# A PEER layer on Trainium2: 160 instead of 128 tokens served by gathered expert rows, and one of the gate products on ScalarE

## The chip, the cores and the metric

The kernel runs on one core of one Trainium2 chip. The metric is device time in microseconds (us) of one execution: the median of three runs of the kernel before is 2171.63 us (2168.15 to 2172.48). A profiled execution of the same kernel gives the trace that is read here.

## The reference, cut to what matters

The reference is one layer of a decoder over 576 tokens that count at the end (512 of a prompt, 64 of eight samples): a gated delta rule and an mLSTM side by side, then a product-key expert layer (PEER), then a norm. The change lies in the expert layer:

```
def block(xb):                                    # 128 tokens
    qh = einsum('td,de->te', xb, w_query).reshape(128, 8, 2, 128)
    s = einsum('thpd,hpnd->thpn', qh, sub_keys)   # 8 heads, 2 halves, 128 keys
    sv, si = top_k(s, 16)
    cand = sv[:, :, 0, :, None] + sv[:, :, 1, None, :]
    top_s, pos = top_k(cand, 16)                  # 16 of 16384 experts a head
    gate = softmax(top_s)
    act = gelu(einsum('thkd,td->thk', expert_u[eidx], xb))
    return einsum('thk,thkd->td', gate * act, expert_v[eidx])
```

Each token picks 8 x 16 = 128 experts; an expert is one row of `expert_u` and one of `expert_v`, 1024 numbers of four bytes each.

## The kernel before

**Two ways for one layer.** Most tokens (ND = 448) go *densely*: TensorE multiplies all 16384 rows of `u` with them, ScalarE takes the Gelu, VectorE multiplies with a gate matrix that is zero for the experts not chosen, and TensorE multiplies the result with all rows of `v`. The last NG = 128 tokens go *by gathered rows*: they lie on the 128 partitions, GpSimd fetches for each the row of its rank-c expert (one indirect DMA of 512 KB a rank, for `u` and again for `v`: 256 gathers), and VectorE takes the dot product with the token (L1225) or adds gate times row to the sum (L1231, tile `yt`).

**The dense loop.** 128 blocks of experts are walked twice, once in `hidden` with `u` (tile `pz`) and once in `experts` with `v` (tile `py`). One step of either loop is called a *half* here: 24 matmuls, that is 8 chunks of D by three products of split numbers (hi by hi, hi by lo, lo by hi: `mm3`, L132 to L134), each with a 128x128 weight and ND columns. Halves 0 to 127 are `hidden`, 128 to 255 `experts`. For each half SP fetches a weight block (`wr`, 512 KB, seven halves ahead), ScalarE makes its high part (`uh`, in `hi`) and VectorE its low part (`ul`, in `lo`); in `hidden` ScalarE takes the Gelu of `pz` (`gz`). In `experts` VectorE multiplies two halves of `gz` with the gates `wj` (L1374) and splits the product (L1381), in alternate halves.

**The gates.** `select` finds the chosen experts of a block of 128 tokens on VectorE, by a long chain of small instructions. `onehots` then builds, for eight tokens (an *octet*, index q), four one-hot arrays `oh[0..3]` of 128 x (8 x 128) on VectorE: two comparisons and two products, high and low part of the gate. `scatter` multiplies them on TensorE with 16 small matmuls (tile `pw`), `stored` copies the result on ScalarE (`wst`) and SP writes it to HBM (`wd`), from where `gates` loads it as `wj`. The array tiles have two buffers each, so octet q needs the matmuls of octet q-2 to be done.

**Order.** From the first half on, PE, DVE, ACT and SP each run strictly in the order in which the program writes their instructions (`in_order`). What VectorE does beside `lo` is dealt out by `fill`: every half gives a credit (HALF less WL for `lo`), from which gathers (1.3 each, as many as `gcred` allows) and pieces of `select` and `onehots` (the number behind `yield`) are paid. Work put off by n halves goes through `later` and `run_due`.

**The end.** After the last half, `gather_out` norms the gathered tokens on VectorE; then the last two blocks of `v` are multiplied one output chunk d at a time, VectorE adds each chunk to `y`, ScalarE squares it and GpSimd adds up five of the squares (`rms_add`), and the dense tokens are normed and written.

## Time and profile before

| | |
|---|---|
| profiled execution, device time | 2175.39 us |
| its span, first to last instruction | 2173.6 us, granted clock 0.986 |
| median of three runs | 2171.63 us |
| TensorE (PE) busy | 2115.0 us, 97% of the span |
| VectorE (DVE) busy | 1561.8 us, 72% |
| ScalarE (ACT) busy | 803.4 us, 37% |
| `hidden`, first matmul to first of `experts` | 807.7 to 1522.6 us |
| `experts`, first to last matmul | 1522.6 to 2157.7 us |

The busy share of PE counts the full length of each matmul, and they overlap; how dense the stream is shows only in the distance from start to start. The shares of DVE, ACT and DMA are means over stages that differ, so they are read by stage.

### The profile page before, as it was taken

The page shows a single profiled execution, that of the slowest core. Times are in us where ns is not written, and L with a number is a line of the kernel's source. Part 1 is how long each engine was busy: PE and PEld are TensorE (multiplying, and loading weights), DVE is VectorE, ACT ScalarE, POOL GpSimd, SP SyncE. Part 2 cuts the span into 40 slices and gives each one's busy share as a digit, 9 for nine tenths or more (in the row PEclk, how much of TensorE's full clock was granted, in tenths as well). Part 3 has the DMA queues.
Part 4 walks back from the last instruction along what each step waited for, and adds up shares of the span by engine and source line. Part 5 has one row for each costly group of instructions (what it writes and reads, how often), then busy time and mean ns, then how long its engine had stood idle before and what let it go on. Part 6 is the DMA issues. An engine that isn't in the chain of part 4 may idle for free.

```text
span 2173.6 us, 33670 instructions
## 1 busy us (share of the span) xinstructions
PE 2115.0 (97%) x12800; PEld 1934.0 (89%) x12800; DVE 1561.8 (72%) x2985; ACT 803.4 (37%) x1217; POOL 539.2 (25%) x423
## 2 busy tenths in 40 slices
PE   8999999999999998999998899999999999999997
PEld 7898999889998998999997799999899999999996
DVE  6676665675557888897885687777887767676764
ACT  5533333343244452334433335433323232323222
POOL 1101000210014552110110121035543334333321
PEclk9999999999999999999999899999999999999999
DMA  6353333556455355767865577789999999999971
GB/s 240 121 161 100 101 104 99 159 158 213 152 163 175 117 193 197 258 209 253 289 232 218 209 246 263 282 313 370 362 387 338 318 330 321 327 320 331 314 259 44
DMA packets 236638, 502.32 MB, mean 231 GB/s; under 512 B 29764, under 2 KB 125764, under 8 KB 232764
## 3 DMA queue, kind: packets, MB, share of 16 engines
q1 hardware_dynamic: 199468, 365.93, 50.0%
q0 software_dynamic: 36864, 134.23, 17.5%
q8 instruction: 100, 1.64, 0.3%
q14 instruction: 62, 0.51, 0.1%
q10 hardware_dynamic: 144, 0.01, 0.0%
HBM read 419.05 MB, written 81.05 MB: 230 GB/s over the span
## 4 chain that ended last, share of the span: by engine, by line
PE 59%; DVE 2%; DMA 0%; issue 0%; ACT 0%; POOL 0%; DVEq 0%; POOLq 0%; ACTq 0%
PE py L132 10%; PE py L134 10%; PE py L133 10%; PE pz L134 9%; PE pz L132 9%; PE pz L133 9%; PE pw L1170 2%; DVE ul L1297 1%; DMA gr<-in_ur,gi 0%; DVE eq L1084 0%; DVE yo L1443 0%; DVE oh L1154 0%; DVE oh L1151 0%; DVE ti L976 0%; DVE ti L980 0%
## 5 line engine op out<-in xcount | busy, mean ns | idle before, releaser
L134 PE MATMUL pz<-x2h,ul 128*128 128x448 f32 x1024 | 380.5, 372 | 19.6 <-DVE ul L1297 19.6
L132 PE MATMUL pz<-x2h,uh 128*128 128x448 f32 x1024 | 384.2, 375 | 0.0
L133 PE MATMUL pz<-x2l,uh 128*128 128x448 f32 x1024 | 379.1, 370 | 0.0
L132 PE MATMUL py<-ah,uh 128*128 128x448 f32 x1024 | 376.3, 368 | 0.6 <-ACT gk L1347 0.6
L133 PE MATMUL py<-al,uh 128*128 128x448 f32 x1024 | 376.2, 367 | 0.0
L134 PE MATMUL py<-ah,ul 128*128 128x448 f32 x1024 | 376.2, 367 | 0.0
L1297 DVE TENSOR_TENSOR ul<-wr,uh 128x1024 fp32r<-128x1024 f32 x256 | 311.9, 1218 | 35.4 <-ACT uh L1291 34.5
L1291 ACT ACTIVATE uh<-wr 128x1024 fp32r<-128x1024 f32 x256 | 269.3, 1052 | 174.9 <-issue 170.2
L1222 POOL DMA_INDIRECT gr<-in_v,gi x128 | 192.4, 1503 | 454.6 <-DVE yt L1231 291.5
L1222 POOL DMA_INDIRECT gr<-in_ur,gi x128 | 188.8, 1475 | 463.4 <-DVE gr L1225 254.1
L132 PE MATMUL acc<-xnh,wh 128*128 128x296 f32 (+1 forms) x768 | 233.6, 304 | 7.2 <-ACT xnh L283 6.2
L133 PE MATMUL acc<-xnl,wh 128*128 128x296 f32 (+1 forms) x768 | 233.9, 305 | 0.5 <-DVE xnl L284 0.5
L134 PE MATMUL acc<-xnh,wl 128*128 128x296 f32 (+1 forms) x768 | 233.1, 305 | 0.0
L134 PEld LDWEIGHTS pz<-x2h,ul 128*128 128x128 f32 x1024 | 195.8, 191 | 39.0 <-DVE ul L1297 22.2
L132 PEld LDWEIGHTS py<-ah,uh 128*128 128x128 f32 x1024 | 191.5, 187 | 21.1 <-ACT gk L1347 1.0
L132 PEld LDWEIGHTS pz<-x2h,uh 128*128 128x128 f32 x1024 | 196.0, 191 | 15.9
L133 PEld LDWEIGHTS pz<-x2l,uh 128*128 128x128 f32 x1024 | 195.8, 191 | 15.5
L134 PEld LDWEIGHTS py<-ah,ul 128*128 128x128 f32 x1024 | 191.5, 187 | 20.1
L133 PEld LDWEIGHTS py<-al,uh 128*128 128x128 f32 x1024 | 191.5, 187 | 20.1
L127 ACT ACTIVATE wh<-wr 128x1024 fp32r<-128x1024 f32 x104 | 110.0, 1058 | 213.5 <-issue 78.1
L1330 ACT ACTIVATE gz<-pz 128x448 f32<-128x448 f32 x118 | 64.1, 543 | 318.6 <-PE pz L134 318.6
L1381 DVE TENSOR_TENSOR al<-gz,ah 128x896 fp32r<-128x896 f32 x59 | 64.5, 1093 | 154.0 <-ACT ah L1376 154.0
(405 smaller groups left out, 3712.9 us busy)
## 6 DMA issues: line engine op xcount, KB each, us to landing
wr<-in_u SPq DMA_DIRECT2D x128, 512.0 KB, 5.6
wr<-in_v SPq DMA_DIRECT2D x128, 512.0 KB, 5.2
gz<-gz SPq DMA_DIRECT2D x112, 448.0 KB, 3.9
wd<-wst SPq DMA_DIRECT2D x28, 1024.0 KB, 6.3
wj<-wd SPq DMA_DIRECT2D x112, 256.0 KB, 5.3
wr<-in_w_in SPq DMA_DIRECT2D x48, 512.0 KB, 3.9
wr<-in_w_q SPq DMA_DIRECT2D x32, 512.0 KB, 3.5
wr<-in_w_out SPq DMA_DIRECT2D x16, 512.0 KB, 4.9
```

Source lines behind the costliest of these rows:

```text
L127: self.last_hi = self.nc.scalar.activation(hi, src, AF.Copy)
L132: mm(out, wh, xh, start=start, stop=False)
L133: mm(out, wh, xl, start=False, stop=False)
L134: self.last_mm = mm(out, wl, xh, start=False, stop=stop)
L1170: nc.tensor.matmul(pw[:, u, :], oh[0][:, t], oh[2 + x][:, t], start=x == 0, stop=x == 1)
L1222: nc.gpsimd.indirect_dma_start(out=t, out_offset=None, in_=src, in_offset=bass.IndirectOffsetOnAxis(ap=self.gi[:, x, c:c + 1], axis=0))
L1291: self.nc.scalar.activation(w, self.raws[s], AF.Copy)
L1297: self.nc.vector.tensor_sub(w, self.raws.pop(s), self.ws[s][0].bitcast(F32))
L1330: nc.scalar.activation(*todo, AF.Gelu)
L1381: nc.vector.tensor_sub(al, z, ah.bitcast(F32))
```

## The change

160 tokens instead of 128 go by gathered rows, 416 instead of 448 densely. The 32 added tokens (NX) lie four times on the partitions; each copy takes a quarter (XK = 32) of the 128 ranks, so 2 x 32 more gathers of 512 KB do it. For this `xt`, `yt`, `gi`, `ga` exist twice; the transposes of `ffn_sink` also bring the 32 tokens into place, four-fold; `select` of block 1 (now tokens 320 to 447) sends its indices to the second `gi` by four SP DMAs; `gather_out` adds up the four partial sums and norms both parts. The low-part gate product `oh[3]` moves from VectorE (one instruction for eight tokens) to ScalarE (eight instructions, one a token, the gate as a scale per partition), at the start of `scatter`, which comes one half after `onehots` instead of two. A ScalarE copy `sx` spreads an operand of the product in `select` over its full size. The weights' high parts are made three halves ahead instead of two. The numbers that set the order change: HALF 4.8 to 4.55 with SCAT 0.9 more in a half that scatters an octet, MUL 1.1 to 1.0, GQ0 (gathers a half in most of `hidden`) 0.65 to 1.1.

```diff
-NG = 128
+NX = 32
+XG = P // NX
+XK = PH * TOPK // XG
+NG = P + NX
-TBLK = [(t, min(P, ND - t)) for t in range(0, ND, P)]
+TBLK = [(NT - 2 * P, P), (0, P), (P, P), (2 * P, NT - 4 * P)]
-HALF = 4.8
-WL, MUL = 1.2, 1.1
+HALF, SCAT = 4.55, 0.9
+WL, MUL = 1.2, 1.0
-GQ0, GQ1, GQ2, GTAIL = 0.65, 2.0, 1.7, 3
+GQ0, GQ1, GQ2, GTAIL = 1.1, 2.0, 1.7, 3
...
@@ ffn_sink
+                for x, (dst, v, a) in enumerate(((self.xt, t, w - NG), (self.yt, self.y[k], ND))):
+                    if k % 2 == 0:
+                        hold[x] = ps.tile([P, 2, 2, P], F32, name=f"xtp{x}", tag=f"xtp{x}")
+                    m = P if x == 0 else NX
+                    nc.tensor.transpose(hold[x][:, 0, k % 2, :], v[:, a + NX:], self.c("ident"))
+                    u = v[:, a:a + NX]
+                    if x == 0:
+                        u = wp.tile([P, P], F32, name="xnr", tag="xnr")
+                        nc.scalar.activation(u.rearrange("p (a b) -> p a b", b=NX), v[:, None, a:a + NX].to_broadcast([P, XG, NX]), AF.Copy)
+                    nc.tensor.transpose(hold[x][:m, 1, k % 2, :], u, self.c("ident"))
...
@@ select
+            sx = wp.tile([P, PH, TOPK, TOPK], BF, name="sbx", tag="cand", bufs=1)
+            nc.scalar.activation(sx[:n], sb[:n, :, :, None].to_broadcast([n, PH, TOPK, TOPK]), AF.Copy)
...
-            nc.vector.tensor_tensor(e[:n], e[:n], sb[:n, :, :, None].to_broadcast([n, PH, TOPK, TOPK]), op=ALU.mult)
-            yield 2.3
+            nc.vector.tensor_tensor(e[:n], e[:n], sx[:n], op=ALU.mult)
+            yield 1.2
...
+            for x in range(XG if b else 0):
+                nc.sync.dma_start(self.gi[1][x * NX:(x + 1) * NX], gi[sl, :, x * XK:(x + 1) * XK])
@@ onehots
-        for x in range(2):
-            nc.vector.tensor_tensor(oh[2 + x], oh[1], rb(2 + x), op=ALU.mult)
-        self.later(2, self.scatter, q, oh)
-        yield 2.75
+        nc.vector.tensor_tensor(oh[2], oh[1], rb(2), op=ALU.mult)
+        self.later(1, self.scatter, q, oh)
+        yield 2.06
@@ scatter
+        self.credit += SCAT
+        for t in range(TG):
+            c = q * TG + t
+            nc.scalar.activation(oh[3][:, t], oh[1][:, t], AF.Copy, scale=self.glo[:, c:c + 1])
@@ gather
-        seq = [("u", 0)] + [x for k in range(1, nrun) for x in (("u", k), ("v", k - 1))] + [("v", nrun - 1)]
+        runs = [(0, k) for k in range(4)] + [(1, k) for k in range(XK // GL)] + [(0, k) for k in range(4, PH * TOPK // GL)]
+        seq = [("u", 0)] + [x for k in range(1, len(runs)) for x in (("u", k), ("v", k - 1))] + [("v", len(runs) - 1)]
...
@@ gather_out
+        for x in range(1, XG):
+            t = self.gp.tile([P, D], F32, name="gr", tag="gr")
+            nc.sync.dma_start(t[:NX], y1[x * NX:(x + 1) * NX])
+            part.append(t)
+        for z, (y, n, o) in enumerate(((y0, P, NX), (y1[:NX], NX, 0))):
+            for t in part if z else ():
+                nc.vector.tensor_add(y, y, t[:NX])
...
@@ hidden, experts
-                self.hi(self.half + 2)
+                self.hi(self.half + 3)
```

Three places in the order of the instructions. **VectorE in `hidden`**, before, about half 62, where the second of two runs of octets begins: rows L1151 to L1154 are one octet, `ul` closes a half.

```order
L1297 TENSOR_TENSOR ul<-wr,uh 128x1024
L1151 TENSOR_TENSOR oh_12085<-iob,rep_12019 128x1024
L1152 TENSOR_TENSOR oh_12086<-iob,rep_12019 128x1024
L1154 TENSOR_TENSOR oh_12087<-oh_12086,rep_12019 128x1024
L1154 TENSOR_TENSOR oh_12088<-oh_12086,rep_12019 128x1024
L1151 TENSOR_TENSOR oh_12095<-iob,rep_12083 128x1024
L1152 TENSOR_TENSOR oh_12096<-iob,rep_12083 128x1024
L1154 TENSOR_TENSOR oh_12097<-oh_12096,rep_12083 128x1024
L1154 TENSOR_TENSOR oh_12098<-oh_12096,rep_12083 128x1024
L1297 TENSOR_TENSOR ul<-wr,uh 128x1024
L1231 SCALAR_TENSOR_TENSOR yt<-gr,ga,yt 128x1024
L1297 TENSOR_TENSOR ul<-wr,uh 128x1024
```

And of the change, in the second run of octets:

```order
L1331 TENSOR_TENSOR ul<-wr,uh 128x1024
L1256 SCALAR_TENSOR_TENSOR yt_5680<-gr,ga_5684,yt_5680 128x1024
L1171 TENSOR_TENSOR oh_12359<-iob,rep_12283 128x1024
L1172 TENSOR_TENSOR oh_12360<-iob,rep_12283 128x1024
L1173 TENSOR_TENSOR oh_12361<-oh_12360,rep_12283 128x1024
L1171 TENSOR_TENSOR oh_12368<-iob,rep_12357 128x1024
L1172 TENSOR_TENSOR oh_12369<-iob,rep_12357 128x1024
L1173 TENSOR_TENSOR oh_12370<-oh_12369,rep_12357 128x1024
L1331 TENSOR_TENSOR ul<-wr,uh 128x1024
```

Before, a half holds no, one or two octets, in the second run in the pattern 2, 0, 1 four times over, in the other two runs always one. In the change 52 octets lie in 36 halves, in three runs: 1, 1, 2, 2, 1, 2, 1, 2; then 1, 1, 2, 2, 2, 1, 1, 2, 2, 1, 1; then 1, 1, 1, 1, 2, 2, 2, 2, 1, 2, 1, 1, 1, 2, 2, 1, 1; a gather stands in nearly each.

**ScalarE in `hidden`**, before, in a run of octets: `gz` is the Gelu, `wst` copies the gates of an octet, `rep` prepares one.

```order
L1330 ACTIVATE gz<-pz 128x448
L1291 ACTIVATE uh<-wr 128x1024
L1178 ACTIVATE wst<-pw 128x128x4 x2
L1135 ACTIVATE rep_13593<-ijg 128x256
L1330 ACTIVATE gz<-pz 128x448
```

And of the change, a half with two octets:

```order
L1364 ACTIVATE gz<-pz 128x416
L1325 ACTIVATE uh<-wr 128x1024
L1201 ACTIVATE wst<-pw 128x128x4 x4
L1183 ACTIVATE oh_12471<-oh_12469,glo 128x128 x8
L1183 ACTIVATE oh_12480<-oh_12478,glo 128x128 x8
L1155 ACTIVATE rep_12579<-ijg 128x192
L1155 ACTIVATE rep_12588<-ijg 128x192
L1364 ACTIVATE gz<-pz 128x416
```

Behind `wst` there now stand eight products an octet (L1183), on which the octet's `pw` matmuls of the same half wait.

**VectorE at the end**, of the change, from the second part of `gather_out` to the first chunk of `y`; before, the rows up to L1276 were not there, and the row before them is the last of the first part in both.

```order
L1270 TENSOR_TENSOR yt_5681<-yt_5681,gr 32x1024 x3
L1273 SCALAR_TENSOR_TENSOR gr,gv<-yt_5681 32x1024
L1274 TENSOR_SCALAR gv<-gv 32x1
L157 RECIPROCAL rsq<-rsq 32x1
L158 TENSOR_TENSOR rst<-rsq 32x1
L159 TENSOR_TENSOR rst<-rst,gv 32x1
L160 TENSOR_SCALAR rst<-rst 32x1
L161 TENSOR_TENSOR gv<-rsq,rst 32x1
L1276 SCALAR_TENSOR_TENSOR gr<-yt_5681,gv,gf 32x1024
L1465 TENSOR_TENSOR yr_16220<-yr_16220,py_16215 128x416
```

Gathers that stand before the low part of half 15: 9 before, 15 now. Gathers that stand before half 128, the first of `experts`: 104 of 256 before, 155 of 320 now, two a half in halves 117 to 127 in both; in halves 128 to 143 there are 28 and 27, from half 150 to 240 1.18 a half before and 1.30 now; the last stands in half 249 in both.

## Rows read from the trace of the kernel before

**Rows 1.** The page: the span, and busy time of each engine with its share and count of instructions.

```profile
span 2173.6 us, 33670 instructions
PE 2115.0 (97%) x12800; PEld 1934.0 (89%) x12800; DVE 1561.8 (72%) x2985; ACT 803.4 (37%) x1217; POOL 539.2 (25%) x423
```

**Rows 2.** The timeline of PE at three places, start us, length us, then line, tiles, columns and count. The first two rows are 105 starts apart (320 columns), the next two 19 starts of the dense loop; then an octet's small matmuls and the first matmuls of the half behind them and of the half after it.

```profile
624.83 0.31 PE L134 MATMUL po<-mh,wl 128*128 128x320 f32 x1
...
640.23 0.31 PE L134 MATMUL po<-mh,wl 128*128 128x320 f32 x1
...
1139.71 0.36 PE L133 MATMUL pz<-x2l,uh 128*128 128x448 f32 x1
...
1143.55 0.37 PE L134 MATMUL pz<-x2h,ul 128*128 128x448 f32 x1
1143.76 1.07 PE L1170 MATMUL pw<-oh,oh 128*128 128x128 f16 x16
1144.64 0.45 PE L132 MATMUL pz<-x2h,uh 128*128 128x448 f32 x1
...
1150.47 0.45 PE L132 MATMUL pz<-x2h,uh 128*128 128x448 f32 x1
```

**Rows 3.** Busy time by stretch: the stretch and its length in us, then busy us of PE, PEld, DVE, ACT and POOL (with the count of instructions that lie in it), the granted clock of TensorE, the DMA engines' busy share and GB/s.

```profile
640.00:660.00 20.00, 18.61 (x135) 15.66 (x134) 14.89 (x31) 12.54 (x22) 1.62 (x2) 1.00 0.54 166
...
808.00:850.00 42.00, 40.64 (x201) 37.06 (x201) 40.46 (x140) 16.92 (x25) 0.25 (x1) 1.00 0.49 171
850.00:900.00 50.00, 45.58 (x208) 41.03 (x207) 43.46 (x114) 15.66 (x20) 22.64 (x16) 0.93 0.81 287
1150.00:1250.00 100.00, 86.18 (x531) 77.05 (x529) 64.17 (x99) 37.09 (x66) 13.08 (x10) 0.88 0.62 222
1470.00:1520.00 50.00, 50.00 (x249) 46.33 (x248) 39.46 (x47) 15.86 (x22) 29.03 (x22) 1.00 1.02 375
...
1600.00:1800.00 200.00, 200.00 (x969) 180.97 (x968) 144.38 (x150) 59.48 (x61) 79.15 (x48) 1.00 0.96 335
```

**Rows 4.** One stall in `hidden`, on PE and on DVE; in brackets the idle time before a row and what ended it.

```profile
1154.57 0.47 PE L134 MATMUL pz<-x2h,ul 128*128 128x448 f32 x1 [3.45 <-DVE ul L1297]
...
1156.39 0.58 PE L134 MATMUL pz<-x2h,ul 128*128 128x448 f32 x1
...
1162.47 0.45 PE L132 MATMUL pz<-x2h,uh 128*128 128x448 f32 x1
```

```profile
1150.77 0.69 DVE L1151 TENSOR_TENSOR oh<-iob,rep 128x1024 f16<-128x1024 f16 x1 [3.21 <-PE pw L1170]
...
1153.30 1.22 DVE L1297 TENSOR_TENSOR ul<-wr,uh 128x1024 fp32r<-128x1024 f32 x1
```

**Rows 5.** DVE at the first gather, after the first `select`, and the two kinds of product of `select` that the change touches (nanoseconds least/median/most, first and last start).

```profile
856.57 1.22 DVE L1225 SCALAR_TENSOR_TENSOR gr<-gr,xt 128x1024 f32<-128x1024 f32 x1 [5.50 <-DMA gr<-in_ur,gi]
```

```profile
L1079 DVE TENSOR_TENSOR eq<-eq,sb x10: 2276/2284/2294, 835.5 to 1279.8; 128x2048 bf16<-128x2048 bf16 x8, 64x2048 bf16<-64x2048 bf16 x2
L1076 DVE TENSOR_TENSOR eq<-ra,io x5: 1208/1215/1217, 834.2 to 1267.7; 128x2048 bf16<-128x2048 bf16 x4, 64x2048 bf16<-64x2048 bf16 x1
```

**Rows 6.** ACT: instructions in a row in `hidden`, and two groups of earlier stages on 128 x 128 numbers, one with an operand per partition (`decay`, its bias `nG`) and one without (`sc`); of `decay` the four that stand in one row as the timeline has them and their single lengths (ns least/median/most, first and last start), of `sc` the lengths.

```profile
1147.65 0.42 ACT L1135 ACTIVATE rep<-ijg 128x256 f16<-128x256 f16 x1 [5.41 <-DVE oh L1154]
1147.98 0.53 ACT L1330 ACTIVATE gz<-pz 128x448 f32<-128x448 f32 x1
1148.40 1.05 ACT L1291 ACTIVATE uh<-wr 128x1024 fp32r<-128x1024 f32 x1
1149.35 1.07 ACT L1178 ACTIVATE wst<-pw 128x512 f32<-128x512 f32 x2
...
1162.29 2.06 ACT L1178 ACTIVATE wst<-pw 128x512 f32<-128x512 f32 x4
```

```profile
207.91 1.28 ACT L576 ACTIVATE decay<-decay,nG 128x128 f32<-128x128 f32 x4 [0.45 <-DVE decay L574]
```

```profile
L576 ACT ACTIVATE decay<-decay,nG x4: 385/386/403, 207.9 to 208.8; 128x128 f32<-128x128 f32 x4
...
L1015 ACT ACTIVATE sc<-psc x80: 263/269/280, 691.2 to 808.9; 128x128 f32<-128x128 f32 x64, 64x128 f32<-64x128 f32 x16
```

**Rows 7.** The end: DVE in `gather_out` and at the first chunk of `y`, GpSimd's five sums, PE's last dense matmul and what follows it.

```profile
2141.08 1.22 DVE L1239 SCALAR_TENSOR_TENSOR gr<-yt 128x1024 f32<-128x1024 f32 x1
...
2143.73 1.29 DVE L1242 SCALAR_TENSOR_TENSOR gr<-yt,gv,gf 128x1024 f32<-128x1024 f32 x1
2149.06 0.62 DVE L1430 TENSOR_TENSOR yr<-yr,py 128x448 f32<-128x448 f32 x1 [4.04 <-PE py L134]
```

```profile
2151.62 6.22 POOL L182 TENSOR_TENSOR rmssum<-rmssum,rmssq 128x448 f32<-128x448 f32 x5 [47.94 <-ACT rmssq L179]
```

```profile
2157.34 0.36 PE L134 MATMUL py<-ah,ul 128*128 128x448 f32 x1
2157.89 0.91 PE L184 MATMUL py<-rmssum,cst 128*1 128x448 f32 x2 [0.20 <-POOL rmssum L182]
```

**Rows 8.** DMA issues: what, queue, count, KB each, median us from issue to landing.

```profile
wr<-in_v SPq DMA_DIRECT2D x128, 512.0 KB, 5.2
...
gz<-gz SPq DMA_DIRECT2D x112, 448.0 KB, 3.9
...
wj<-wd SPq DMA_DIRECT2D x112, 256.0 KB, 5.3
```

More of the change, by code (lines that the diff above doesn't have):

```diff
@@ L235, in build @@
             with self.pool("y") as yp:
-                self.xt = yp.tile([P, D], F32, name="xt")
-                self.yt = yp.tile([P, D], F32, name="yt")
-                self.gi = yp.tile([P, 2, PH * TOPK], I32, name="gi")
-                self.gg = yp.tile([P, PH * TOPK], F32, name="gg")
-                self.ga = yp.tile([P, PH * TOPK], F32, name="ga")
+                self.xt = [yp.tile([P, D], F32, name=f"xt{x}") for x in range(2)]
+                self.yt = [yp.tile([P, D], F32, name=f"yt{x}") for x in range(2)]
+                self.gi = [yp.tile([P, 3, n], I32, name=f"gi{x}") for x, n in enumerate((PH * TOPK, XK))]
+                self.ga = [yp.tile([P, n], F32, name=f"ga{x}") for x, n in enumerate((PH * TOPK, XK))]
                 with self.pool("x2") as xp:
@@ L941, in merge @@
                     nc.vector.tensor_tensor(self.y[e][:, o:o + w], x[:, :w], po[:, :w], op=ALU.add)
-                self.norm(o, w, "norm_ffn", self.ffn_sink(o, w, ps3), ps2, ps2, wp)
+                self.norm(o, w, "norm_ffn", self.ffn_sink(o, w, ps3, wp), ps2, ps2, wp)
             for k in range(KC):
@@ L954, in norm, with ffn_sink @@
             sink(k, t)
-    def ffn_sink(self, o, w, ps):
+    def ffn_sink(self, o, w, ps, wp):
         nc = self.nc
         hold = {}
+        if o + w == NT:
+            nc.gpsimd.memset(self.yt[1], 0.0)
         def sink(k, t):
@@ L1030, in scored @@
                 if o == 0:
-                    for s in range(2):
+                    for s in range(3):
                         self.fetch(s)
                         self.hi(s)
-                        self.lo(s)
+                        if s < 2:
+                            self.lo(s)
                 scores(*prev)
@@ L1133, in spread @@
             return
-        r = self.rep[q] = self.wp.tile([P, 4, TG, 8], F16, name="rep8", tag="rep8")
-        self.nc.scalar.activation(r, self.ijg[:, :, q * TG:(q + 1) * TG, None].to_broadcast([P, 4, TG, 8]), AF.Copy)
+        r = self.rep[q] = self.wp.tile([P, 3, TG, 8], F16, name="rep8", tag="rep8")
+        self.nc.scalar.activation(r, self.ijg[:, :, q * TG:(q + 1) * TG, None].to_broadcast([P, 3, TG, 8]), AF.Copy)
     def onehots(self, q, last):
@@ L1236, in gather_out @@
         nc = self.nc
-        t = self.gp.tile([P, D], F32, name="gr", tag="gr")
-        v = self.gp.tile([P, 1], F32, name="gv", tag="gv", bufs=1)
-        nc.vector.scalar_tensor_tensor(t, self.yt, 1.0, self.yt, op0=ALU.mult, op1=ALU.mult, accum_out=v)
-        nc.vector.tensor_scalar(v, v, 1.0 / D, EPS, op0=ALU.mult, op1=ALU.add)
-        self.rsqrt(v, self.gp, bufs=1)
-        nc.vector.scalar_tensor_tensor(t, self.yt, v, self.gf, op0=ALU.mult, op1=ALU.mult)
-        nc.sync.dma_start(self.O["yg"], t)
+        y0, y1 = self.yt
+        part = []
+        for x in range(1, XG):
[5 more added lines that the diff above has]
+                nc.vector.tensor_add(y, y, t[:NX])
+            t = self.gp.tile([P, D], F32, name="gr", tag="gr")[:n]
+            v = self.gp.tile([P, 1], F32, name="gv", tag="gv", bufs=1)[:n]
+            nc.vector.scalar_tensor_tensor(t, y, 1.0, y, op0=ALU.mult, op1=ALU.mult, accum_out=v)
+            nc.vector.tensor_scalar(v, v, 1.0 / D, EPS, op0=ALU.mult, op1=ALU.add)
+            self.rsqrt(v, self.gp, bufs=1)
+            nc.vector.scalar_tensor_tensor(t, y, v, self.gf[:n], op0=ALU.mult, op1=ALU.mult)
+            nc.sync.dma_start(self.O["yg"][o:o + n], t)
     def after(self, ins, anchor):
@@ L1264, in fill @@
         while self.credit > 0:
-            if self.gready and self.gcred >= 1 and self.gstep < 2 * PH * TOPK:
+            if self.gready and self.gcred >= 1 and self.gstep < 2 * (PH * TOPK + XK):
                 self.gcred -= 1
@@ L1309, in hidden @@
         self.routing = self.route()
-        for s in range(2, 7):
+        for s in range(3, 7):
             self.fetch(s)
@@ L1406, in experts @@
                     self.fetch(self.half + 7)
-                    self.hi(self.half + 2)
+                    self.hi(self.half + 3)
                     if h == 0:
@@ L1419, in experts @@
                         nc.sync.dma_start(self.y[d], self.yd[:, d, :])
-            while self.gstep < 2 * PH * TOPK:
+            while self.gstep < 2 * (PH * TOPK + XK):
                 self.gather()
```

58 lines of the change are left out of this document (30 added, 28 removed).

## The prediction, made before the changed kernel ran

> **What bounds the kernel now.** I read first the busy times [rows 1]: PE is busy for 97% of the span. Whether it is at its pace shows in the distances from start to start. In `hidden`, 19 starts with 448 columns take 3.84 us, 0.2025 each [rows 2]. In `experts`, 200 us hold 969 starts, 0.2064 each, with PE busy all of the 200 us and a granted clock of 1.00 [rows 3]; the first and last matmul of `experts` give the same: 635.1 us for 128 x 24. So `experts` is a stream without gaps. An octet costs PE 0.97 more: a half with 16 `pw` matmuls takes 5.83 [rows 2], without them 24 x 0.2025 = 4.86. With 56 octets `hidden` is 3072 x 0.2025 + 56 x 0.97 = 676.4 of its 714.9 us; 38.5 are lost.
>
> Two losses can be seen. In the second run of octets two octets stand before `ul` in one half (the order above); the second needs the `pw` matmuls of the half before. DVE idles 3.21 for `pw`, `ul` starts at 1153.30, PE idles 3.45, and its matmuls run at 0.58 for some time, the granted clock of this stretch being 0.88 [rows 4, 3]. This half takes 12.00 us; with two octets 4.86 + 1.94 = 6.80 would do: 5.2 lost, and the pattern 2, 0, 1 brings it four times, 20.8 in all. The other: at the first gather DVE waits 5.50 us for data [rows 5], and the clock falls to 0.93 [rows 3]. The rest, about 12, is small waits at the start, where DVE is busy 40.46 of 42 us [rows 3], and the slower pace of some halves.
>
> ACT has room everywhere on average (37%), but the order is fixed, so the halves with octets must be looked at singly. The DMA engines are full where gathers come two a half: share 1.02 at 375 GB/s, with PE busy 50.00 of 50 us [rows 3].
>
> **The change part by part.**
>
> *448 to 416 columns.* The length in proportion to 0.2025 is 0.1880; the line from 320 columns (105 starts in 15.40 us, 0.1467 [rows 2]) to 448 gives 0.1885. I take 0.188 for `hidden`. For `experts`, 0.2064 gives 0.1917 in proportion and 0.1915 by the line; I take 0.192, and 0.188 as the bound if the faster pace returns. The same 128x128 weights already run at 0.1467, so loading weights is no floor at these lengths. `hidden`: 3072 x 0.0145 = -44.5, and four octets fewer x 0.97 = -3.9. `experts`: 3072 x (0.2067 - 0.192) = -45.2.
>
> *Order of the octets.* `scatter` one half after `onehots`, and no half in which an octet needs a `pw` of the half before that hangs on this half's `ul`: -20.8 (bounds -10 and -24).
>
> *`oh[3]` on ACT.* This is the doubtful part, since eight products per octet stand on ACT behind `wst`, and the `pw` of that half and then the next `gz` and `uh` wait for them. No row shows this operation in f16 with a scale per partition. Nearest is `decay`, 128x128 with an operand per partition: 0.386 each, but four in 1.28 us, so behind the first one 0.298 from start to start [rows 6]. `sc`, 128x128 without such an operand, has 0.269 alone [rows 6]; two of these products could overlap more, and half of `decay`, 0.157, is my lower bound (`wst`, 4 x 512 columns in 2.06 us, and `rep`, 256 columns at 0.33, give about 0.15 for 128 of a longer row [rows 6]). The upper bound is 0.386, no overlap. I take 0.293, just under the 0.298, since `decay` has the same shape and kind of operand and the row of products is twice as long. Per octet ACT then has wst 0.95 (2 of the 0.475 a row) + 8 x 0.293 = 2.34 + rep 0.28 (192 of 256 columns) = 3.57; per half also uh 0.95 and gz 0.42 [rows 6], 1.37. A half with one octet: ACT 4.94, PE 24 x 0.188 + 0.97 = 5.48. With two: ACT 8.51, PE 6.45, so ACT is 2.06 late. The order has 16 double and 20 single halves. If nothing is made good, 16 x 2.06 = 33; if each single half gives back its 0.54, 22. Going through the order half by half, with `uh` made three halves ahead as the only slack, I get 29. Idle PE also lost clock in the stall above (about 1.75 of the 5.2); here the gaps are shorter, and I add 5 (bounds 0 and 28). Sum +34. At 0.157 a double half has ACT 6.3 against 6.45: 0 to 5. At 0.386 it is 10.0 in double, 5.69 in single halves: 16 x 3.56 + 20 x 0.21 = 61, with the clock 66.
>
> A sentence on the skill: the Trainium skill, in "ScalarE: Activation LUTs", Rules for kernel authors, sends plain multiplication to VectorE and budgets about 0.3 us for an ACTIVATE with a pointer operand plus 0.83 ns an element, which would make 0.41 us of each product, and of the sum (same working, 16 x 3.9 + 20 x 0.4 + 5) about 76 instead of 34, an estimate from that page; the row of `decay` speaks against it, as four of them took 1.28 and not 1.6.
>
> What the edit saves DVE: one product of about 0.62 (its `oh` row is 0.69 with its start [rows 4]) and, in `select`, 2.28 less about 1.21 [rows 5], five blocks twice. After the first gather this is hidden behind PE. Ahead of it DVE sets the pace: PE would gain nine halves x 0.345 = 3.1, DVE saves about 1.5 net of new small pieces, so 1.6 of the gain is lost: +1.6. A spread `sx` on ACT lies under DVE's other work there (ACT busy 16.92 of 42 [rows 3]).
>
> *64 more gathers.* 1.2 us of DVE each [rows 5], 77 in all; DVE has 55 idle of each 200 us of `experts` [rows 3]: hidden. The order has 15 instead of 9 gathers before `ul` of half 15, while GpSimd and the DMA engines have just begun: +1.5 (0 to 6). As traffic: a gather and a weight block are 0.524 MB each [rows 8]. At two gathers a half plus `gz` and `wj` (0.213 MB each; only from half 138 both): halves 117 to 127 ask 1.786 MB in 4.51 us, 396 GB/s; 138 to 143 1.835 in 4.61, 398; from 144 on 1.632, 354. At the 375 seen [rows 3] the first eleven take 4.76 and the six 4.89, that is 2.8 + 1.7 = 4.5; blocks are fetched seven halves ahead, so I take +3 (0 to 10).
>
> *The front and the end.* 16 more transposes, at most 0.1467 each, behind which are ACT copies where ACT is busy 12.54 of 20 us [rows 3]: +2 (0 to 5). `gather_out` took DVE from 2141.08 to 2145.02, 3.94 us [rows 7]; three adds as long as a `ul` (1.22 [rows 4]) and a second norm come to it: 7.6 more. DVE was idle 4.04 before the first chunk of `y` [rows 7], so this starts some 3.5 late. GpSimd's five sums (6.22 us) are behind it and end at 2157.84, 0.2 before PE's last work begins [rows 7]: this delay reaches the end almost whole, +3 (0 to 5). The four DMAs to the second `gi` stand on SP in one half, with blocks seven halves ahead behind them: 0.
>
> **Sum.** `hidden` -44.5 - 3.9 - 20.8 + 34 + 1.6 + 1.5 = -32.1; `experts` -45.2 + 3 = -42.2; front and end +5. From the profiled 2175.4: 2106.1. The profiled execution is 3.8 above the median, so 2102.
>
> **Rivals.**
> *The products are cheap* (0.157 to 0.2): 34 becomes about 5, 2073. For it: short ACT instructions overlap. Against: `decay`.
> *No overlap* (0.386): 66 for 34, 2134. The page's rule above belongs here (2144 by its figure).
> *DMA limits.* If 335 GB/s, the mean of steady `experts` [rows 3], were the ceiling, halves from 144 would take 4.87 for 4.61, 106 x 0.26 = 28, those before some 15 more: 2145. Against: 375 was reached without an idle PE.
> *A new wait* of another kind in the hot halves or at the first gathers, such as DVE's order there, with `ul` behind two octets and a gather (six of 0.62 and two of 1.2: 6.1 against PE's 6.45): if DVE became the later one by 1 us in 16 halves with the clock as in [rows 4], 25 more: 2127.
> *Slower.* ACT products must cost so much that 34 becomes 103: with 52 octets in 36 halves the loss is 52 x (1.23 + 8a - 0.97) - 36 x 3.14 + 5, which reaches 103 at a = 0.475 us a product. All rows are below it; f16 operands are the one reason for which it could be.
> *No change* would need the pace not to fall with the columns; 0.1467 at 320 against 0.2025 speaks against it.
>
> **How the numbers follow.** Main case 0.49 (2088 to 2116 with its bounds); cheap products 0.22; no overlap 0.09; DMA 0.05; new wait 0.10; slower 0.03; no change 0.02. The time is the main case's, 2102. The range takes in the cheap case but for its lowest end, and the no-overlap case: 2066 to 2134. Runs can tell about 0.2% (4 us) from no change. Faster by more 0.95, same 0.02, slower 0.03.
>
> **What would show it.** Start to start 0.188 of `pz` and 0.192 of `py`, and `experts` near 590 to 593 us. No idle of 3 us before `ul` near half 64. On ACT eight L1183 products in 2.3 us; idle of PE before `pw`, put down to ACT, in halves with two octets, about 2 us each, and `hidden` near 683. The last sums of GpSimd about 3 us later behind the last matmul. The forecast is wrong above all if L1183 isn't near 0.293, if `uh` three ahead gives no slack (more wait in double halves), or if `py` keeps another pace than its columns say.

## The result, and the profile after

The changed kernel takes 2090.8 us (median of four, 2085.5 to 2094.3), the kernel before on the same chip 2170.5: a ratio of 0.963, 95% interval 0.961 to 0.966. It is faster, by 80 us; 2102 was forecast, with 2066 to 2134 as the range. The profiled execution has 2085.5 us, against the 2175.4 of before: 89.9 us between the two. The profiled one of after is the fastest of its four, and that of before lies above all four of its own, so some 10 of the 89.9 us are spread between executions. The stages, read as before, share them like this (us):

| stage | before | after | change | forecast |
|---|---|---|---|---|
| up to the first matmul of `hidden` | 807.7 | 805.0 | -2.7 | +2 |
| `hidden` | 714.9 | 674.8 | -40.1 | -32.1 |
| `experts`, to the last dense matmul | 635.1 | 574.2 | -60.9 | -42.2 |
| from there to the end of the span | 15.9 | 29.8 | +13.9 | +3 |
| span | 2173.6 | 2083.7 | -89.9 | -69.3 |

The sum is near, but three of its terms are not, and they partly cancel. The page of after, the lines that answer to [rows 1]:

```profile
span 2083.7 us, 34219 instructions
PE 2020.4 (97%) x12752; PEld 1930.9 (93%) x12752; DVE 1587.6 (76%) x3026; ACT 925.5 (44%) x1654; POOL 585.0 (28%) x488
```

The share of PE is 97% as before, and says nothing of what changed. Busy time by stretch of after, which answers to [rows 3] (columns as there):

```profile
850.00:900.00 50.00, 43.11 (x213) 41.37 (x212) 39.52 (x86) 13.29 (x19) 29.11 (x22) 0.93 0.99 366
1030.00:1080.00 50.00, 49.16 (x355) 44.70 (x353) 41.56 (x73) 47.04 (x126) 9.31 (x9) 0.97 0.83 297
...
1452.00:1500.00 48.00, 47.39 (x254) 47.04 (x253) 41.28 (x53) 17.75 (x23) 30.26 (x20) 1.00 1.04 389
1600.00:1800.00 200.00, 200.00 (x1072) 199.90 (x1071) 166.12 (x180) 65.19 (x68) 75.64 (x58) 1.00 1.03 376
```

In `experts` 200 us now hold 1072 matmuls, 0.1867 each; 969 stood there before. ACT is busy 47.04 of 50 us in a run of octets (second line). ACT in one half with two octets, after:

```profile
1038.65 0.50 ACT L1364 ACTIVATE gz<-pz 128x416 f32<-128x416 f32 x1
1039.05 1.05 ACT L1325 ACTIVATE uh<-wr 128x1024 fp32r<-128x1024 f32 x1
1040.00 2.05 ACT L1201 ACTIVATE wst<-pw 128x512 f32<-128x512 f32 x4
1041.91 4.79 ACT L1183 ACTIVATE oh<-oh,glo 128x128 f16<-128x128 f16 x16
1046.58 0.38 ACT L1155 ACTIVATE rep<-ijg 128x192 f16<-128x192 f16 x1
```

Sixteen products take 4.67 us from start to start of the next row, 0.292 each. Their single lengths (ns least/median/most):

```profile
L1183 ACT ACTIVATE oh<-oh,glo x416: 386/415/484, 1021.0 to 1374.1; 128x128 f16<-128x128 f16 x139
```

And what PE does meanwhile:

```profile
1041.70 0.23 PE L1193 MATMUL pw<-oh,oh 128*128 128x128 f16 x1
1042.39 4.63 PE L1193 MATMUL pw<-oh,oh 128*128 128x128 f16 x31 [0.46 <-ACT oh L1183]
1046.78 0.70 PE L135 MATMUL pz<-x2h,uh 128*128 128x416 f32 x1
1047.27 0.55 PE L136 MATMUL pz<-x2l,uh 128*128 128x416 f32 x1
```

The small matmuls of two octets, 1.94 us of work, last from 1041.70 to 1046.78, since two of them at a time wait for a token's product. Little of that counts as idle time: it is hidden in the modelled length of the group. Behind it the next dense matmuls are 0.55 long for a while instead of 0.35; the granted clock of these 5 us is 0.81 (columns as in [rows 3]):

```profile
1047.00:1052.00 5.00, 5.00 (x24) 4.89 (x24) 3.87 (x6) 5.00 (x13) 1.15 (x1) 0.81 0.92 252
```

Not every half with two octets loses the same. Halves 46, 67, 92 and 101, behind halves with one, take 6.5 us and lose nothing; the halves right behind them, with two octets again, take 9.67 to 9.73 and lose 3.2 to 3.3.

The end of after, DVE, GpSimd and PE, which answers to [rows 7]:

```profile
2040.49 1.22 DVE L1331 TENSOR_TENSOR ul<-wr,uh 128x1024 fp32r<-128x1024 f32 x1 [1.72 <-PE py L137]
...
2045.49 3.69 DVE L1270 TENSOR_TENSOR yt<-yt,gr 32x1024 f32<-32x1024 f32 x3
...
2053.00 4.05 DVE L1465 TENSOR_TENSOR yr<-yr,py 128x416 f32<-128x416 f32 x8
```

```profile
2054.73 5.62 POOL L185 TENSOR_TENSOR rmssum<-rmssum,rmssq 128x416 f32<-128x416 f32 x5 [46.43 <-ACT rmssq L182]
```

```profile
2060.41 1.55 PE L187 MATMUL py<-rmssum,cst 128*1 128x416 f32 x2 [6.46 <-POOL rmssum L185]
2061.75 2.98 PE L187 MATMUL py<-rmssq,cst 128*1 128x416 f32 x4
```

All eight chunks of `y` are ready or nearly so when DVE comes to them at 2053.00; PE's last dense matmul began at 2053.60. PE then waits 6.46 where it waited 0.20, and the `rmssum` matmuls take 1.55 where they took 0.91. The granted clock of that stretch is 1.00 before and 0.50 after, that is 2.4 and 1.2 GHz; before and after:

```profile
2157.80:2161.00 3.20, 2.42 (x6) 0.41 (x6) 1.18 (x3) 0.58 (x1) 0.04 (x1) 1.00 0.00 0
```

```profile
2060.40:2066.00 5.60, 4.92 (x9) 1.19 (x10) 0.59 (x2) 0.00 (x0) 0.00 (x0) 0.50 0.00 0
```

### The profile page after: what moved, and what is told of

It reads as the page before. It is cut to its first block, busy times and chain, and to the rows that moved or that the text cites. A ratio compares the mean times of both kernels' runs of the same rounds, so it can differ in the third digit from the quotient of the medians.

```text
span 2083.7 us, 34219 instructions
## 1 busy us (share of the span) xinstructions
PE 2020.4 (97%) x12752; PEld 1930.9 (93%) x12752; DVE 1587.6 (76%) x3026; ACT 925.5 (44%) x1654; POOL 585.0 (28%) x488
## 3 DMA queue, kind: packets, MB, share of 16 engines
q8 instruction: 100, 1.64, 0.3%
## 4 chain that ended last, share of the span: by engine, by line
PE 54%; DVE 3%; issue 1%; ACT 1%; DMA 1%; POOL 0%; DVEq 0%; ACTq 0%; POOLq 0%
PE py L135 9%; PE py L137 9%; PE py L136 9%; PE pz L135 8%; PE pz L137 8%; PE pz L136 8%; PE pw L1193 3%; DMA gr<-in_ur,gi 1%; DVE ul L1331 1%; ACT wst L1201 0%; ACT uh L1325 0%; POOL gr L1247 0%; POOL rmssum L185 0%; PE py L187 0%; DVE ti L992 0%
## 5 line engine op out<-in xcount | busy, mean ns | idle before, releaser
L137 PE MATMUL pz<-x2h,ul 128*128 128x416 f32 x1024 | 361.2, 353 | 10.3 <-DVE ul L1331 10.3
L135 PE MATMUL pz<-x2h,uh 128*128 128x416 f32 x1024 | 364.4, 356 | 0.0
L136 PE MATMUL pz<-x2l,uh 128*128 128x416 f32 x1024 | 360.5, 352 | 0.0
L135 PE MATMUL py<-ah,uh 128*128 128x416 f32 x1024 | 356.7, 348 | 0.6 <-ACT gk L1381 0.6
L137 PE MATMUL py<-ah,ul 128*128 128x416 f32 x1024 | 357.0, 349 | 0.0
L136 PE MATMUL py<-al,uh 128*128 128x416 f32 x1024 | 356.8, 348 | 0.0
L1247 POOL DMA_INDIRECT gr<-in_ur,gi x160 | 211.5, 1322 | 402.7 <-DVE gr L1250 208.9
L1247 POOL DMA_INDIRECT gr<-in_v,gi x160 | 213.0, 1331 | 379.3 <-DVE yt L1256 235.4
L1256 DVE SCALAR_TENSOR_TENSOR yt<-gr,ga,yt 128x1024 f32<-128x1024 f32 x160 | 205.1, 1282 | 6.2 <-DMA gr<-in_v,gi 4.5
L1250 DVE SCALAR_TENSOR_TENSOR gr<-gr,xt 128x1024 f32<-128x1024 f32 x160 | 192.7, 1219 | 12.6 <-DMA gr<-in_ur,gi 12.5
```

The costliest lines, as they stand in the source:

```text
L135: mm(out, wh, xh, start=start, stop=False)
L136: mm(out, wh, xl, start=False, stop=False)
L137: self.last_mm = mm(out, wl, xh, start=False, stop=stop)
L1247: nc.gpsimd.indirect_dma_start(out=t, out_offset=None, in_=src, in_offset=bass.IndirectOffsetOnAxis(ap=gi[:, x, c:c + 1], axis=0))
L1250: nc.vector.scalar_tensor_tensor(t, t, 1.0, xt, op0=ALU.mult, op1=ALU.mult, accum_out=ga[:, c:c + 1])
L1256: nc.vector.scalar_tensor_tensor(yt, t, ga[:, c:c + 1], yt, op0=ALU.mult, op1=ALU.add)
```

## The experiments

### One gate product: back on VectorE

```
-            nc.scalar.activation(oh[3][:, t], oh[1][:, t], AF.Copy, scale=self.glo[:, c:c + 1])   # x8, in scatter
+            nc.vector.tensor_tensor(oh[3], oh[1], rb(3), op=ALU.mult)                             # in onehots
```

With it `rep` spreads four parts again instead of three.

> The changed kernel with one edit undone: oh[3] on VectorE again, one product of 0.62 us an octet, nothing of it on ScalarE; the order is else the same. Theory (the 30 us are ScalarE's 8.5 us in halves with two octets): now VectorE is the later one there, with eight of 0.62, ul and a gather 7.4 us against 6.45, about 0.9 in 16 halves, so 30 becomes some 15 and the whole gains about 15 us. Rival (the waits come from scatter standing one half after onehots, whoever makes the product): within 5 us of the changed kernel. Rival (the move to ScalarE pays): 5 us or more slower.

Measured: 2070.5 us (2069.5 to 2072.4), 0.953 of before (0.951 to 0.955), 20 us less than the changed kernel. `hidden` is 654.9 instead of 674.8. PE in two halves with two octets each:

```profile
1042.27 1.96 PE L1191 MATMUL pw<-oh,oh 128*128 128x128 f16 x32
1048.65 1.96 PE L1191 MATMUL pw<-oh,oh 128*128 128x128 f16 x32
```

The 32 small matmuls take 1.96 again, and the two groups are 6.38 us apart, about what PE needs (24 x 0.1867 + 1.94). Seven of the 36 halves with octets take 7.1 to 8.3 us, all of them behind another half with two octets or soon after it: around the longest, half 73, VectorE works without a gap and takes 7.4 us for the eight instructions of two octets, `ul` and a gather. So the loss in the halves with octets (their length less 4.52 less 0.97 an octet, summed) falls from 30.5 to 8 us. The loss is that of the products on ScalarE, not of the earlier `scatter`; by this run the edit that moves them costs 20 us in this order of the octets.

### At most one octet in a half

```
+            if self.octet == self.half:                # set in onehots
+                self.credit = min(self.credit, 1.0)
+                return
             c = next(self.routing, None) if self.routing else None
-GQ0 = 1.1
+GQ0 = 0.85
```

(The line that sets `self.octet` and the other numbers in the line of `GQ0` are left out here.)

> The changed kernel, with at most one octet in a half (52 halves with one instead of 36 with one or two) and, so that all octets still fit, 0.85 instead of 1.1 gathers a half in most of hidden. Theory (ScalarE is too slow only in halves with two octets): the 30 us that the halves with octets take beyond 4.52 + 0.97 an octet fall to under 4, hidden to about 648 us, the whole gains 24 to 28 us. Rival A (the products on ScalarE make TensorE wait in every half with an octet, or the loss is VectorE's): under 10 us gained. Rival B (the gathers that are put off to experts meet the DMA engines' limit): experts rises above its 574 us.

Measured: 2068.3 us (2066.5 to 2068.7), 0.952 of before (0.950 to 0.954), 22.5 less than the changed kernel. `hidden` is 643.1. PE, the small matmuls of three halves in a row:

```profile
1297.06 1.07 PE L1194 MATMUL pw<-oh,oh 128*128 128x128 f16 x16
...
1302.55 1.07 PE L1194 MATMUL pw<-oh,oh 128*128 128x128 f16 x16
...
1307.99 1.07 PE L1194 MATMUL pw<-oh,oh 128*128 128x128 f16 x16
```

5.49 and 5.44 apart: with ScalarE making all products, a half with one octet takes just what PE needs. So the halves with two octets, and those right behind them, made the loss. But rival B was there too: `experts` rose to 583.6. Two stretches of it, and all waits of PE from 1500 to 2000 (`al` is the low part of the split product of Gelu and gates):

```profile
1500.00:1600.00 100.00, 100.00 (x537) 99.95 (x536) 86.36 (x99) 33.04 (x34) 57.46 (x35) 1.00 1.04 390
...
1700.00:1800.00 100.00, 97.60 (x522) 96.85 (x521) 89.17 (x101) 33.44 (x35) 60.40 (x35) 1.00 1.05 388
```

```profile
PE py L136 <- DVE al L1420: 6.4, 5, 1.9
```

At 390 GB/s, share 1.04 to 1.05, the DMA engines are full; five times, in halves 168, 184, 200, 216 and 232, `al` is late and PE waits for it. Ahead of the wait in half 184 VectorE itself has waited for a load:

```profile
1700.95 1.03 DVE L1413 TENSOR_TENSOR gz<-gz,wj 128x832 f32<-128x832 f32 x1 [7.78 <-DMA wj<-wd]
```

Why it is every 16th half isn't shown.

### The end

```
-            self.gather_out()                                     # behind the loop
+                    if 2 * NK - 6 < self.half < 2 * NK - 3:       # in the loop: first part, second part
+                        self.gather_out(self.half - 2 * NK + 5)
```

> The changed kernel, with gather_out taken out of the end: its first part stands in half 251, its second in half 252, right behind the last gathers, where VectorE has over 2 us idle in each half. Theory (the adds and the second norm stand on VectorE ahead of the first chunk of y, and the last ul comes a half later than before since ul has three buffers): the time from the last dense matmul to the end of the span falls from 29.8 to about 15.5 us, TensorE no longer waits 6.5 us for rmssum, and the whole gains 13 to 14 us. Rival (the end is longer by itself, by 416 columns or by a lower clock): less than 3 us gained.

Measured: 2087.8 us (2081.9 to 2092.4), 0.960 of before (0.957 to 0.963); 3 less than the changed kernel, which its own spread doesn't tell from nothing. The mechanism was there and the gain was eaten: PE waits only 0.35 for `rmssum`, and from the last dense matmul to the end are 20.6 us instead of 29.8. But `experts` is 5 us longer. DVE in half 252:

```profile
2047.00 3.71 DVE L1273 TENSOR_TENSOR yt<-yt,gr 32x1024 f32<-32x1024 f32 x3 [1.32 <-DMA gr<-yt]
2050.74 1.21 DVE L1276 SCALAR_TENSOR_TENSOR gr<-yt 32x1024 f32<-32x1024 f32 x1
...
2054.51 1.01 DVE L1419 TENSOR_TENSOR al<-gz,ah 128x832 fp32r<-128x832 f32 x1
```

and PE behind it:

```profile
2055.57 0.71 PE L136 MATMUL py<-al,uh 128*128 128x416 f32 x1 [3.45 <-DVE al L1419]
```

The second part, 7.5 us in one piece, now stands ahead of `al`, for which PE waits 3.45 and then runs at 0.71 a matmul. A stall that is moved asks again what is queued behind it.

### Both

The two edits above together (with 0.85 gathers).

> The changed kernel with both: gather_out in halves 251 and 252, and at most one octet in a half with 0.85 gathers. Theory: the gains add up, 37 to 42 us, about 2050 us. If the DMA engines are the limit in experts, 5 to 15 us less of it.

Measured: 2068.5 us (2062.2 to 2069.7), 0.951 of before (0.948 to 0.953): nothing beyond the single octets alone. The end is 20.0 us, 9 less; `experts` is 589.1, 5.5 more, by the wait just shown on top of the full DMA engines; the stages ahead of `hidden` took 7 us longer in this execution, in code that is the same.

### The order of the octets, alone in the kernel before

```
-        self.later(2, self.scatter, q, oh)
+        self.later(1, self.scatter, q, oh)
```

> The kernel before with one edit of the change alone: scatter one half after onehots instead of two. Theory (in the run with the pattern 2, 0, 1 the second octet of a half waits for pw matmuls that stand behind the next dense half, and ul behind it): the four halves of 12.0 to 13.1 us near half 64 to 73 become 6.8, hidden falls from 714.9 to 692 to 696, the whole gains 18 to 24 us. Rival (the stall is VectorE's amount of work in a half with two octets, not the order): the four halves stay above 9 us and under 8 us are gained.

Measured: 2127.0 us (2122.8 to 2128.5), 0.979 of before (0.977 to 0.980): 44.5 us, twice what was expected. `hidden` is 686.6, 28 less: the four halves took 12.0, 12.9, 13.1 and 13.1 and take 6.7 each, 24.2 us together. That part was right. The other 20 us are in `experts`, 614.7 instead of 635.1, where nothing was edited. The stretch of the four halves, and one of `experts`:

```profile
1150.00:1250.00 100.00, 100.00 (x620) 91.99 (x619) 84.66 (x170) 45.13 (x74) 21.66 (x12) 1.00 0.79 279
1600.00:1800.00 200.00, 200.00 (x1002) 187.69 (x1001) 148.99 (x164) 62.57 (x64) 80.86 (x50) 1.00 0.97 342
```

1002 matmuls of 448 columns in 200 us, where the kernel before had 969 [rows 3]: 0.200 instead of 0.2064, with PE busy without a gap and the granted clock at 1.00 in both. So 448 columns have two paces.

### The pace by columns

```
-                            self.mm3(py[d][:, :ND], wh[:, d, :], wl[:, d, :], ah[:, h], al[:, h], self.half == NK, False)
+                            x = (k - NP - 4) // 10
+                            n = ND - 16 * x if 0 <= x < 5 else ND
+                            self.mm3(py[d][:, :n], wh[:, d, :], wl[:, d, :], ah[:, h, :n], al[:, h, :n], self.half == NK, False)
```

> The kernel before, in which the matmuls of experts take fewer columns in some stretches (10 pairs of halves each with 432, 416, 400, 384 of the 448, then 448 again; the products of the columns left out are missing from the result). It measures start to start by columns, with all else as before. If the pace goes by the columns in proportion (as the prediction took it): 0.199, 0.192, 0.185, 0.177. If it is the columns plus 32 at the 2.4 GHz level, as 320 columns (0.1467) and the 416 of the changed kernel (0.1867) are: 0.193, 0.187, 0.180, 0.173, and 448 with 0.2067 instead of 0.200 is the odd one.

Measured in one execution (2126.8 us), stretches with 448, 432, 416, 400, 384 and again 448 columns (columns as above; a count includes up to two matmuls that lie partly outside):

```profile
1550.00:1650.00 100.00, 100.00 (x486) 90.54 (x485) 77.88 (x84) 29.84 (x31) 45.19 (x28) 1.00 1.02 374
1660.00:1750.00 90.00, 90.00 (x452) 84.19 (x451) 67.61 (x74) 27.96 (x29) 34.87 (x22) 1.00 0.97 337
1760.00:1840.00 80.00, 80.00 (x430) 79.99 (x429) 64.22 (x75) 26.78 (x28) 35.12 (x22) 1.00 1.01 363
1845.00:1925.00 80.00, 80.00 (x441) 80.00 (x440) 65.49 (x67) 26.75 (x27) 33.96 (x22) 1.00 1.01 359
1932.00:2012.00 80.00, 80.00 (x464) 80.00 (x463) 70.68 (x72) 27.85 (x29) 37.37 (x24) 1.00 1.04 381
2020.00:2100.00 80.00, 80.00 (x402) 75.12 (x401) 52.86 (x53) 24.16 (x25) 15.54 (x9) 1.00 0.53 187
```

From the first to the last start of each: 0.2067, 0.2000, 0.1867, 0.1822, 0.1733, and at last 0.2000 for the same 448. Neither guess is right for all. 416, 384 and the later 448 are the columns plus 32 at 2.4 GHz; 448 at first and 432 are the columns plus 48, 400 plus 37. The proportion, on which the forecast for `experts` rested, is not how it goes, and a number of columns has more than one pace.

### What changes the pace

Small matmuls (64 columns into a part of a PSUM bank that nothing reads) between the halves of `experts`, in the kernel before:

```
+                    for x in range({150: 1, 170: 1, 190: 1, 210: 16}.get(self.half, 0)):
+                        nc.tensor.matmul(py[7][:, ND:], self.c("ident"), self.c("ident")[:, :64], start=True, stop=True, skip_group_check=True)
```

> The kernel before with one small matmul (64 columns, into a part of the PSUM bank that nothing reads) ahead of halves 151, 171 and 191 of experts and 16 of them ahead of half 211. In hidden the pace of 448 columns went from 0.2067 to 0.2025 at the first small matmuls of an octet and stayed. If the pace is set by how the stream of matmuls starts, py goes to about 0.2025 behind one of these places, and experts becomes 3 to 12 us shorter. If it belongs to the form of py (eight banks in turn, its operands), it stays at 0.2067 and experts at 635 us.

Measured: one execution of 2155.4 us (the small matmuls disturb its result, so it serves for its times alone); `experts` 622.6. Before and behind the first place:

```profile
1530.00:1630.00 100.00, 100.00 (x487) 90.55 (x486) 81.39 (x90) 30.28 (x32) 49.85 (x32) 1.00 1.03 378
1640.00:1740.00 100.00, 100.00 (x503) 93.84 (x502) 73.37 (x83) 30.28 (x32) 40.09 (x25) 1.00 0.95 334
```

0.2067 before, 0.200 after, and so to the end; the other places changed nothing. The expected 0.2025 was not the pace that came. The same with a single one, behind the first half of `experts`:

```
+                    for x in range({128: 1}.get(self.half, 0)):
```

> The kernel before with one small matmul (64 columns, into a part of the PSUM bank that nothing reads) behind the first half of experts and nothing else. In the run with four such places py went from 0.2067 to 0.200 at the first and stayed there. If a single disturbance of the stream sets the pace, and in every execution: experts falls from 635 to 615 or 616 us, and the whole gains 18 to 21 us, as much as the pace gave the changed kernel beyond its fewer columns. If it was chance in one execution, or if this place leaves the pace as it is: within 4 us of before.

Measured: 2153.4 us (2148.5 to 2153.6), 0.991 of before (0.988 to 0.994), that is 19 us for one matmul that computes nothing. `experts` 615.0:

```profile
1600.00:1800.00 200.00, 200.00 (x1002) 187.69 (x1001) 148.99 (x157) 62.14 (x64) 81.53 (x50) 1.00 0.98 348
```

Its four executions lie within about 5 us, so this isn't chance in one of them.

### GpSimd's last instruction

The span of after ends 6 us behind its last DMA, that of before 1.5. What lies there is a DRAIN of GpSimd; its durations (ns least/median/most, the longest is the one meant) before and after:

```profile
L1529 POOLq DRAIN  x3: 40/102/5383, 2166.6 to 2173.4; - x3
```

```profile
L1564 POOLq DRAIN  x3: 40/102/10505, 2072.4 to 2083.5; - x3
```

The changed kernel without its last 64 gathers:

```
         self.gstep += 1
+        if s >= 256:
+            return GU
```

> The changed kernel without its last 64 gathers (256 instead of 320, as many as before; the products of the last ranks are missing from the result), all else in the same order. GpSimd's last instruction, a DRAIN, took 5.39 us in all kernels with 256 gathers and 10.51 in all with 320, and ends the span. If its length goes by the number of gathers: 5.4 us again, the end 5 us shorter. If it goes by another part of the change: 10.5 us. Either way experts stays at 574 us, since its gathers lie beside TensorE's work.

Measured: one execution of 2087.2 us, with 677.0 in `hidden` and 574.3 in `experts`, where the changed kernel has 674.8 and 574.2; from the last dense matmul to the end 24.4 instead of 29.8. The DRAIN:

```profile
L1566 POOLq DRAIN  x3: 40/102/5280, 2078.6 to 2085.2; - x3
```

So its length goes with the gathers: 5 us more for 64 more. (The last gather starts at 1791.6 here and at 2101.8 in the kernel before, so it isn't how late it stands.) What it does in that time the rows don't show.

### A version from these, and two edits of it

At most one octet in a half (`GQ0` 0.95, `HALF` 4.65); of `gather_out` the sums of the second part in halves 221, 223 and 225, its norm in 227 (its ranks are gathered early), the first part in 251.

> The changed kernel with at most one octet in a half (0.95 instead of 1.1 gathers a half in most of hidden, credit of a half 4.65 instead of 4.55), and with gather_out taken apart: the three sums of the second part in halves 221, 223 and 225, its norm in 227, the first part in 251, so that no half holds more than 4 us of it. Theory: no ScalarE wait in hidden (about 645 us), fewer gathers left for experts than with 0.85, so that the DMA engines stay under the 390 GB/s seen (experts 574 to 578), the end 16 to 18 us; about 2050 us. If the gathers still meet that ceiling, experts is 580 to 585.

Measured: 2053.8 us (2047.6 to 2056.5), 0.945 of before (0.943 to 0.947), 37 us less than the changed kernel. `hidden` 645.1, `experts` 574.2, end 21.0. In `experts`:

```profile
1500.00:1600.00 100.00, 100.00 (x537) 99.95 (x536) 85.96 (x96) 33.63 (x35) 54.51 (x34) 1.00 1.04 391
1600.00:1700.00 100.00, 100.00 (x537) 99.95 (x536) 87.70 (x98) 32.45 (x34) 54.87 (x34) 1.00 1.05 388
```

PE never waits there at 391 GB/s: with the gathers spread a little more, the engines are full and nothing is so late that PE waits for it. The end, 21.0 us, stays above the 16 to 18 expected, since the DRAIN is 10.51 us long here too.

The same with `oh[3]` on VectorE:

> The version with at most one octet in a half and gather_out taken apart, with oh[3] back on VectorE (one product of 0.62 us an octet). Theory: with one octet in a half ScalarE needs 4.9 of 5.48 us and VectorE, with its product back, 4 x 0.62 + 2.4 = 4.9, so neither is late and it makes no difference which of them has it: within 5 us of the 2053.8. Rival (VectorE has no room left): 8 us or more slower.

Measured: 2053.0 us (2049.3 to 2058.3), 0.944 of before (0.941 to 0.947): no difference. Where each half of `hidden` has one octet, neither engine is late, and the product may be on either. In `experts` of the profiled execution PE waits once, 2.19 us for `al` in half 240 (1.36 in that of the next version), behind a wait of VectorE for a load of 7.52 (7.40): at this rate the DMA engines leave little room.

The same with small matmuls behind halves 16, 52, 87 and 112:

> The version with at most one octet in a half and gather_out taken apart, with one small matmul (64 columns) behind halves 16, 52, 87 and 112 of hidden, where its pz stood at 0.190 instead of 0.1867 (halves 8 to 61 and 87 to 127). If a small matmul always brings the quicker of the two paces: some 0.08 us a half behind each place, hidden falls from 645 to 638 to 641 and the whole gains 4 to 7 us. If it does so only sometimes, or only for the matmuls of experts: pz stays at 0.190 behind most places and the time within 4 us of 2053.8.

Measured: 2051.2 us (2047.6 to 2057.7), 0.944 of before (0.942 to 0.945): within its spread of the 2053.8. `hidden` was 647.0 in the profiled execution. There a half without an octet went from 4.48 to 4.52 us behind half 52 (from 0.1867 to a mixture of 0.190 and 0.183, 0.1883 on the mean), the wrong way; behind halves 16, 87 and 112 it stayed at 4.52. So the expected 0.08 us a half was twice what lies between the two paces, and the place at half 52 is read from one execution only. A small matmul doesn't always bring the quicker pace, and the 19 us of the kernel before are no recipe.

## Why the prediction was right, and where it was not

**Columns in `hidden`**: taken as 0.188; halves without an octet and without a wait take 4.52 us (0.1883 a matmul), most of them up to half 64, or 4.48 (0.1867), those of 77 to 87 and of 106 to 126 among them. By 0.1883 it is -43.6 for -44.5, and -3.9 for four octets. Right. (The 0.2025 from which it started is a half's 4.86 us by 24; the 19 starts in 3.84 us that it names for it give 0.2021.)

**The order of the octets**: -20.8 taken, 24.2 by the kernel before with this edit alone. Right; the other three halves were worse than the one that was read, by 3.4 us together.

**The products on ScalarE**: 0.293 taken from `decay`, 0.292 measured, though each row is 0.415 long. The page's budget (the Trainium skill, "ScalarE: Activation LUTs", Rules for kernel authors), about 0.41, is the single length here, and not the price in a row. The loss was +34 in the sum and 30.5 in the halves with octets, the lower clock behind them included. The 29 of the forecast comes from a walk through the order half by half that it doesn't print, so only its result can be compared; a half with two octets loses 0.0 to 3.3 us, and not 2 each. The undone edit shows that the waits are ScalarE's, and puts the net loss of the move at 20, since 8 are lost with the product back on VectorE.

**The other losses of `hidden`**: 17.7 were left as they were and 3.1 added, 20.8; what 674.8 holds beyond 3072 x 0.1883, 52 x 0.97 and the 30.5 is 15.4. Of these 5.4 us less, 3.4 are the other three halves just named, which the forecast had left among the 17.7. The wait for the first gather is 4.88 for 5.50 [rows 5], as the row of DVE has it; halves 13 and 14, with the early gathers, lose 2.6 for the 1.5 taken:

```profile
853.51 1.29 DVE L1250 SCALAR_TENSOR_TENSOR gr<-gr,xt 128x1024 f32<-128x1024 f32 x1 [4.88 <-DMA gr<-in_ur,gi]
```

**Columns in `experts`**: the step that failed. `0.2064` was taken as the pace of 448 columns and cut in proportion to 0.192, -45.2. It is 0.1867, and the stage has -60.9. Of these, 41 are the columns (3072 x (0.200 - 0.1867); 614.7 of the one kernel less 574.2 gives the same 40.5), and 20 are the slower of two paces, in which the kernel before stood and the changed one doesn't stand. The forecast saw both paces, 0.2025 and 0.2064, and took the second for a property of the stage, with the first as a bound. The bound of 0.188 came near the truth, but 0.1867 is 4 us beyond it; the proportion itself did not hold. Why the kernel before stood at 0.2067 stays open.

**DMA**: +3 taken for six halves and eleven, 0 measured: 389 to 391 GB/s were served without a wait of PE. So 375, the rate read before the change, was no ceiling, and neither was 335, that rival's. No run moved more than 392 GB/s over 100 us, and in the version with 0.85 gathers loads were late at 388 to 390.

**The end**: +3 taken, +13.9 measured; the second step that failed, in three places. The work itself was right: VectorE's from `ul` to the first chunk takes 11.4 us, where 3.94 + 7.6 were taken. The working took the slack of 4.04 us from the trace of before and added 7.6 us of work to it. But the last `ul` stands later now: 13.1 us ahead of the start of the last dense matmul (2040.49 to 2053.60) and behind a wait for PE (`1.72 <-PE py`). Before, DVE's row of it was this, 17.4 ahead of the last dense matmul [rows 7]:

```profile
2139.95 1.22 DVE L1297 TENSOR_TENSOR ul<-wr,uh 128x1024 fp32r<-128x1024 f32 x1
```

`ul` has three buffers now and not four, an edit of one word that the forecast passed over. The 4.3 us between 17.4 and 13.1 are about one half (4.48), which fits one buffer less; no run with four buffers tests it. So the first add came 6.9 us late (its chunk was ready at 2046.1, the last one's end less seven times 1.12) and not 3.5. The second place is the clock: behind PE's 6.46 idle us it stands at 0.50, and the three groups of small matmuls that follow take 4.33, 1.64 and 2.22 us, where they took 2.43, 1.04 and 1.31, 3.4 more together. With `gather_out` moved into the loop the wait is 0.35 and the end 9.2 shorter, which is most of these two. The third place is the DRAIN, 5 us, of which no row of before gave a hint.

**Front**: +2 taken. Up to the last matmul of `acc` (an earlier stage), in code that is the same, the profiled execution was 5.1 us quicker, behind it 2.4 slower. That fits the +2, but doesn't show it: such differences of a few us between executions are in all the kernels here, so single stages ahead of `hidden` aren't to be compared closer.

Of the rivals, cheap products (0.157), no overlap (0.386) and a DMA ceiling of 335 are excluded by the rows above. The new wait for VectorE in the hot halves didn't come: from half 17 to 127 PE has no wait above 0.15 us for `ul`. The prediction was right in its direction, and right in mechanism for `hidden`. That its total came so near is in part luck: against the forecast stand +11 at the end, -19 in `experts`, -8 in `hidden` and -5 ahead of it.

## What to carry to other kernels

A pace is read at more than one place before it is scaled: where one form of matmul stands at two paces in the same trace, the difference is a term of its own. An average that leaves an engine half idle hides the halves in which it is the slowest; with a fixed order it pays to sum each engine for each step, and to give a step no more than the slowest can do. A smaller number of buffers may move an instruction as a new line of code does, and slack must be read from where it will stand.
